# Block 0's gate moves its split halves to the MLP ring; the norms of blocks 2 and 3 are woven into the stages before the MLP; two key buffers and larger rings of small tiles

## The chip, the cores and the metric

The kernel runs on one core of a Trainium2 chip. The metric is device microseconds of one execution. A core has a matrix engine (PE, with its weight loads shown apart as PEld), three engines for elementwise work (VectorE: DVE, ScalarE: ACT, GpSimd: POOL) and a queue that issues all of this kernel's data transfers (SyncE: SP). Each of them works through its own list of instructions strictly in the order in which the list was written; they meet only in semaphore waits. On-chip memory (SBUF) holds tiles of 128 partitions; PSUM holds matmul results.

## What is computed

One layer of a streaming encoder for 2048 prompt frames and 32 sample frames of width 1024: an RMS norm, one input projection, two kinds of attention, an output projection with a residual, an MLP, a gate, a final norm. The part that the change touches:

```python
oa = diff_core(q, k, v, bias, mask, lam)    # 4 heads, two maps of 64 dims, softmax over all earlier keys
h = h + concat(oa, ob) @ w_out              # "outproj"
c = rmsnorm(h, g_mlp)                       # "cnorm", its row factor r is "colnorm"
h = h + square(relu(c @ w_up)) @ w_down     # "mlp"
h = h + sigmoid(h @ w_ple_gate) * (p @ w_ple_proj)   # "gate"
y = rmsnorm(h, g_final)                     # "final"
```

All of it is in 32-bit floats. Every matmul operand is split into a high part in the matrix engine's own 32-bit format and a remainder in the same format, and each product is made of three matmuls (high by high, high by low, low by high).

## The kernel before, in words

Activations lie transposed (features on partitions, tokens along the free side). The 2080 tokens are cut into four blocks: 0, 1 and 2 of 512 tokens, 3 of 544 in two pieces of 272. Blocks 0 and 1 make the first half, 2 and 3 the second. Intermediate results go through device memory: `kS` (split keys), `qS`, `oT` (attention output), `xT` (the input), `hS` (the residual stream after the output projection), `rS` (the row factors of the norm).

Weights come through `wunit` (L177): one transfer into a raw tile `wr` (a ring of two buffers), a copy to the high part `wh` on ACT (L169), a subtraction for the low part `wl` on POOL in four pieces of 256 columns (L164, L154), with rings of three. `split` (L165) does the same to activations; `mm3` (L185) issues the three matmuls per term, on L190, L191 and L192.

The order of the work. The Python text emits instructions in program order, with generators woven into each other by `weave` (one step of a side job after each step of the main job). A planner then lists the instructions of each engine: it goes through a simulated time, and whenever an engine is free it takes the ready instruction that stands first in the program. What it lists is fixed before the run. Where a transfer on the chip takes longer than the planner took it to take, the engine waits at that place of its list although later entries could run. Tiles of one tag share a ring of `bufs` buffers.

The stages that matter here, in program order:

- `attn_a` for the key groups `JA1` (L512). For each of four heads (g) it loads the keys of that head into `ka` (one buffer of 2208 columns, two maps; six transfers), and then works through the query pairs j: (4, 5) for all four heads, and then (6, 7, 8) for all four; j = 8 is the sample, whose 160 keys are the last columns of `ka`. Scores `s` come from L567.
- The MLP of blocks 0 and 1 (`mlp`, L976), which stands behind the attention in the program, and which the planner puts into the places where the matrix engine would wait for the attention. `oload(2)` (L822) reads and splits the attention output of block 2 into the 16 buffers of the ring `up`, and can start when the attention's memory is free.
- `gate(1)` (L996) and `final(1)`.
- `outproj(2)` (L844) woven with `oload(3)`; `outproj(3)`, with the row factor of block 2 (`colnorm`, L889) after its first step. A step of `outproj` is one weight unit: it loads `hd` from `xT`, adds the matmul result (L860), squares it on ACT (L865), adds the squares on POOL, and stores `hd` to `hS`. `hd`, the squares, the raw attention output and the raw rows of the norm all share the tag `tmp`, a ring of four.
- `gate(0)`: its split of h lies in two large tiles `hH`, `hL` of the ring `act` (four large tiles in all, which the split attention output of block 3 and the normed blocks 2 and 3 also use). After its first step the row factor of block 3 is made.
- `cnorm(2)`, `cnorm(3)` (L870): load r back from `rS`, and for each of eight row groups load `hS`, scale (DVE, L881), and split (copy on ACT, low part on POOL or DVE in turn) to `cH`, `cL`.
- The MLP of blocks 2 and 3 with `final(0)` between; its first part computes for each of two column groups f the blocks 2 and 3 (`mlp_up`, L917). Then the last gates and norms.

Of the kernel before, what the change touches and what calls it, by code (L numbers as in the profile page):

```python
# [19 lines left out]
P = 128  # L20
D = 1024
# [61 lines left out]
def drain(gen):  # L83
    for _ in gen:
        pass
# [48 lines left out]
class Kern:  # L134
    def __init__(self, tc, a):
        self.tc = tc
        self.nc = tc.nc
        self.a = a

    def dma(self, dst, src):  # L140
        if dst.dtype == F32R:
# [34 lines left out]

    def wunit(self, src, shape, hi_eng="act", lo_eng="pool"):  # L177
        nc = self.nc
        raw = self.wp.tile([P] + shape, F32, tag="wr", bufs=2, name="wr")
        self.dma(raw, src)  # L180
        hi = self.wp.tile([P] + shape, F32R, tag="wh", bufs=3, name="wh")
        lo = self.wp.tile([P] + shape, F32R, tag="wl", bufs=3, name="wl")
        self.split(hi, lo, raw, hi_eng, lo_eng)
        return hi, lo
# [326 lines left out]
    def attn_a(self, js, pool, ps_s, ps_t, ps_o):  # L511
        nc = self.nc  # L512
        last = 8 in js
        nk = KC if last else 256 * (js[-1] + 1)
        for g in range(4):
            ba = self.bias_a(pool, g)
            kt = pool.tile([P, 2, 1024 if self.small else KC], F32R, tag="ka", bufs=1, name="ka")
            for hl in range(2):
                src = self.kS[g, hl].rearrange("(m r) c -> r m c", m=2)
                for c0 in range(0, nk, 1024):  # L520
                    c1 = min(c0 + 1024, nk)
                    self.dma(kt[64 * hl : 64 * hl + 64, :, c0:c1], src[:, :, c0:c1])
            for j in js:
                self.attn_a_pair(g, j if j < 8 else None, kt, ba, pool, ps_s, ps_t, ps_o)

    def attn_a_pair(self, g, j, kt, ba, pool, ps_s, ps_t, ps_o):
        nc = self.nc
# [9 lines left out]
        for qi, t in enumerate(tiles):  # L537
# [25 lines left out]
            for bi, (k0, n, near) in enumerate(blocks):  # L563
                for m in range(2):
                    s = ps_s.tile([P, 512], F32, tag="s", name="s")[:nr, :n]
                    for hl in range(2):
                        nc.tensor.matmul(  # L567
                            s, q[:, m, hl, P * qi : P * qi + nr], kt[:, m, k0 : k0 + n], start=hl == 0, stop=hl == 1
                        )
                    dst = e[m][:nr, k0 - kb : k0 - kb + n]  # L570
                    nmx = nm[:nr, m, bi : bi + 1]
                    if near is None:
                        nc.vector.tensor_reduce(nmx, s, axis=AX.X, op=ALU.max, negate=True)  # L573
                        src = s
                    else:
                        nc.vector.tensor_tensor_reduce(
                            dst, s, ba[:nr, near : near + n], 1.0, -3e38, ALU.add, ALU.max, nmx
                        )
                        nc.vector.tensor_scalar(nmx, nmx, -1.0, None, op0=ALU.mult)
                        src = dst  # L580
                    nc.scalar.activation(dst, src, AF.Exp, bias=nmx, accum_out=z[:nr, m, bi : bi + 1])  # L581
# [218 lines left out]
                self.dma(self.pS[:, 1, k, t0 : t0 + n], lo[:, :n])  # L800

    def raw_o(self, wk, k, t0, n):
        t = wk.tile([P, BLK], F32, tag="tmp", bufs=4, name="oraw")[:, :n]
        self.dma(t, self.oT[:, k, t0 : t0 + n])
        return t

# [34 lines left out]
    def outproj(self, b, wk, oact, ps, acc):  # L841
        nc, a = self.nc, self.a
        n, t0 = BN[b], 512 * b
        W = a["w_out"][0]  # L844
        sq = wk.tile([P, BLK], F32, tag="acc", bufs=2, name="sqacc2")[:, :n]
        acc.append(sq)
        for d in range(8):
            wh, wl = self.wunit(W[:, P * d : P * d + P].rearrange("(k p) c -> p k c", p=P), [8, P])
            h = wk.tile([P, BLK], F32, tag="tmp", bufs=4, name="hd")[:, :n]
            self.dma(h, self.xT[:, d, t0 : t0 + n])  # L850
            for s0, sn in SUBS[b]:
                p = ps.tile([P, 512], F32, tag="mm", name="ops")[:, :sn]
                self.mm3(
                    p,
                    [
                        (wh[:, k], wl[:, k], oact[0][k][:, s0 : s0 + sn], oact[1][k][:, s0 : s0 + sn])
                        for k in range(8)
                    ],
                )
                nc.vector.tensor_tensor(h[:, s0 : s0 + sn], h[:, s0 : s0 + sn], p, op=ALU.add)  # L860
            if d == 0:
                nc.scalar.activation(sq, h, AF.Square)
            else:
                tmp = wk.tile([P, BLK], F32, tag="tmp", bufs=4, name="tmp")[:, :n]
                nc.scalar.activation(tmp, h, AF.Square)  # L865
                self.pool_tt(sq, sq, tmp, ALU.add)
            self.dma(self.hS[:, d, t0 : t0 + n], h)
            yield

    def cnorm(self, b, wk, act, out):  # L870
        nc = self.nc
        n, t0 = BN[b], 512 * b
        cH = act.tile([P, 8, act.aw], F32R, tag="act", name="cH")
        cL = act.tile([P, 8, act.aw], F32R, tag="act", name="cL")
        out[b] = (cH, cL)
        r = wk.tile([P, BLK], F32, tag="r", bufs=2, name="rl")[:, :n]
        self.dma(r, self.rS[:, t0 : t0 + n])
        for k in range(8):
            tmp = wk.tile([P, BLK], F32, tag="tmp", bufs=4, name="tmp")[:, :n]
            self.dma(tmp, self.hS[:, k, t0 : t0 + n])  # L880
            nc.vector.scalar_tensor_tensor(  # L881
                tmp, tmp, self.g_mlp[:, k : k + 1], r, op0=ALU.mult, op1=ALU.mult
# [34 lines left out]
    def mlp_up(self, ch, nf, blocks, st, wk, up, mm):  # L917
        nc = self.nc
        Wu = self.a["w_up"][0]
        us = {}  # L920
        for f in range(nf):
            ft = nf * ch + f
            wh, wl = self.wunit(Wu[:, P * ft : P * ft + P].rearrange("(k p) c -> p k c", p=P), [8, P])
            for b in blocks:
                h, cH, cL = st[b]
                uh = up.tile([P, up.aw], F32R, tag="u", name="uh")
                ul = up.tile([P, up.aw], F32R, tag="u", name="ul")
                us[f, b] = (uh, ul)
                for s0, sn in SUBS[b]:
                    ps = mm.tile([P, 512], F32, tag="mm", name="ups")[:, :sn]  # L930
                    self.mm3(
                        ps,
                        [(wh[:, k], wl[:, k], cH[:, k, s0 : s0 + sn], cL[:, k, s0 : s0 + sn]) for k in range(8)],
                    )
                    r = wk.tile([P, BLK], F32, tag="tmp", bufs=4, name="relu")[:, :sn]
                    nc.scalar.activation(r, ps, AF.Relu)  # L936
                    nc.scalar.activation(r, r, AF.Square)
                    self.split(uh[:, s0 : s0 + sn], ul[:, s0 : s0 + sn], r, "act", "pool")
        return us

    def mlp_down(self, ch, nf, blocks, us, st, wk, mm):
# [43 lines left out]
        self.gf = pool.tile([P, D], F32, name="gf")  # L985
        self.dma(self.gf, self.a["g_final"].unsqueeze(0).broadcast_to([P, D]))

    def gate(self, b, h, up, act, md):
        nc, a = self.nc, self.a
        n, t0 = BN[b], 512 * b  # L990
        Wg, Wp = a["w_ple_gate"][0], a["w_ple_proj"][0]
# [1 line left out]
        for i in range(2):  # L993
            for k in range(2):
                self.dma(pT[i][k][:, :n], self.pS[:, i, k, t0 : t0 + n])
        hH = act.tile([P, 8, act.aw], F32R, tag="act", name="hH")  # L996
        hL = act.tile([P, 8, act.aw], F32R, tag="act", name="hL")
        for k in range(8):
            self.split(hH[:, k, :n], hL[:, k, :n], h[:, k, :n], "act", "dve" if k % 2 else "pool")
        for dq in range(2):  # L1000
            ph, pl = self.wunit(
                Wp[:, 512 * dq : 512 * dq + 512].rearrange("(k p) c -> p k c", p=P), [2, 512]
# [1 line left out]
            for d4 in range(4):  # L1004
                d = 4 * dq + d4
                wh, wl = self.wunit(Wg[:, P * d : P * d + P].rearrange("(k p) c -> p k c", p=P), [8, P])
                for s0, sn in SUBS[b]:
                    pg = md.tile([P, 512], F32, tag="mm", name="gps")[:, :sn]
                    self.mm3(
                        pg,  # L1010
                        [(wh[:, k], wl[:, k], hH[:, k, s0 : s0 + sn], hL[:, k, s0 : s0 + sn]) for k in range(8)],
                    )
                    sg = up.tile([P, BLK], F32, tag="u", name="sig")[:, :sn]
                    sm = up.tile([P, BLK], F32, tag="u", name="sm")[:, :sn]
                    nc.scalar.activation(sg, pg, AF.Abs)
                    nc.vector.tensor_scalar(sm, pg, 0.0, None, op0=ALU.min)
                    nc.scalar.activation(sg, sg, AF.Exp, scale=-1.0)
# [78 lines left out]
    def run(self):  # L1096
        tc, nc, a = self.tc, self.nc, self.a
        with ExitStack() as top:
# [8 lines left out]
            cp = opened(top, "cp", 1)  # L1107
            self.dp = opened(top, "dp", 1, bass.MemoryType.DRAM)
            self.wp = opened(top, "wp", 3)
            mm = opened(top, "mm", MM, PSUM)  # L1110
            tp = mm
            psx = ExitStack()
# [84 lines left out]
                weave(self.outproj(1, wk, oa[1], mm, acc[1]), norms(0, actq, mm), 1, 1)  # L1197
            hq = opened(sq_, "hq", 1)
            uq = Sized(opened(sq_, "uq", 8), 512)
            up = Sized(opened(top, "uh", 16, side="right"), BLK)  # L1200
            oxs = ExitStack()
            ox = opened(oxs, "ox", 1, side="right")

# [21 lines left out]
            psx.close()  # L1225
            wk = opened(top, "wk4", 1)
            fk = opened(top, "fk4", 1)
            self.gfin(fk)
            md = opened(top, "md", 8 - MM, PSUM, "right")
            act = Sized(opened(top, "acth", 4), BLK, True)  # L1230
# [1 line left out]
            weave(self.outproj(2, wk, oa[2], md, acc[2]), self.oload(3, wk, act, oa), 1, 0, OW)  # L1232
            g = self.outproj(3, wk, oa[3], md, acc[3])
            next(g)
            self.colnorm(acc[2][0], 2, 1.0 / D, wk, mm, "mm", self.rS)
            drain(g)
            h = hload(hh, BLK, 0)
            g = self.gate(0, h, up, act, md)
            next(g)
            self.colnorm(acc[3][0], 3, 1.0 / D, wk, mm, "mm", self.rS)  # L1240
            drain(g)
            for b in HALVES[1]:
                drain(self.cnorm(b, wk, act, cn))
            f = self.final(0, h, up, fk, mm)
            st = {b: (hload(hh, BLK, b),) + cn[b] for b in HALVES[1]}
            m = self.mlp(HALVES[1], st, wk, up, mm, md)
# [59 lines left out]
```

## Time and profile before

| what | value |
|---|---|
| median of 3 runs | 3257.93 us (3256.7 to 3264.15) |
| the profiled execution's own time | 3256.49 us |
| its span, first to last instruction | 3254.6 us |
| granted matrix-engine clock, mean | 0.984 |
| PE busy | 3076.7 us, 95% of the span |
| POOL, ACT, DVE busy | 52%, 52%, 48% |
| DMA moved | 489 MB, mean 150 GB/s |
| key attention `JA1` with the MLP of blocks 0 and 1 | about 1260 to 2100 us |
| gate(1), final(1), outproj(2), outproj(3), gate(0), norms | about 2109 to 2374 us |
| MLP of blocks 2 and 3 | about 2359 to 3115 us |

The span and the execution's time differ by 1.9 us, which lies before the first and after the last instruction. A line of a wait table reads: engine, what it was about to do and its line, what released it, the total in us, how many times, and the longest. A line of a table by windows gives the stretch, its length, and the busy time and instruction count of PE, PEld, DVE, ACT and POOL, then the mean granted clock, the DMA share and GB/s. A timeline line gives start, length, engine, line, operation, output and inputs, count, and in brackets the idle time before it with its releaser. Times on "issue" are those where the profile shows no releaser.

### The profile page before, as it was taken

The page shows a single profiled execution, that of the slowest core. Times are in us where ns is not written, and L with a number is a line of the kernel's source. Part 1 is how long each engine was busy: PE and PEld are TensorE (multiplying, and loading weights), DVE is VectorE, ACT ScalarE, POOL GpSimd, SP SyncE. Part 2 cuts the span into 40 slices and gives each one's busy share as a digit, 9 for nine tenths or more (in the row PEclk, how much of TensorE's full clock was granted, in tenths as well). Part 3 has the DMA queues.
Part 4 walks back from the last instruction along what each step waited for, and adds up shares of the span by engine and source line. Part 5 has one row for each costly group of instructions (what it writes and reads, how often), then busy time and mean ns, then how long its engine had stood idle before and what let it go on. Part 6 is the DMA issues. An engine that isn't in the chain of part 4 may idle for free. (4 is left out here: it accounts for less than half of the span.)

```text
span 3254.6 us, 51557 instructions
## 1 busy us (share of the span) xinstructions
PE 3076.7 (95%) x17881; PEld 2692.7 (83%) x17881; DVE 1557.3 (48%) x3952; ACT 1693.7 (52%) x3717; POOL 1706.8 (52%) x2515
## 2 busy tenths in 40 slices
PE   6998999899999999999999999989899999999998
PEld 6877789789987887878788788868789999999988
DVE  5116786544465554676664565625442232223235
ACT  4226666776666765676665566544443222322245
POOL 5446766233245544565655455676854333433387
PEclk9999999999999999999999999999999999999999
DMA  7488786786788654554644544347531111111133
GB/s 232 165 259 246 226 244 206 213 259 202 215 239 229 187 146 118 152 156 138 199 122 135 137 123 136 121 143 233 150 113 46 46 46 46 46 46 46 47 94 103
DMA packets 519085, 489.02 MB, mean 150 GB/s; under 512 B 37885, under 2 KB 414017, under 8 KB 518825
## 3 DMA queue, kind: packets, MB, share of 16 engines
q1 hardware_dynamic: 518824, 485.73, 50.9%
q8 instruction: 142, 2.33, 0.3%
q14 instruction: 119, 0.97, 0.1%
HBM read 379.06 MB, written 110.49 MB: 150 GB/s over the span
## 5 line engine op out<-in xcount | busy, mean ns | idle before, releaser
L164 POOL TENSOR_TENSOR wl<-wr,wh 128x256 fp32r<-128x256 f32 x936 | 695.2, 774 | 489.4 <-ACT wh L169 453.1
L169 ACT ACTIVATE wh<-wr 128x1024 fp32r<-128x1024 f32 x338 | 357.2, 1057 | 598.5 <-PE dps L191 298.9
L971 DVE TENSOR_TENSOR h<-h,dps 128x512 f32<-128x512 f32 (+1 forms) x640 | 373.0, 585 | 575.0 <-PE dps L192 562.7
L154 POOL TENSOR_TENSOR wl<-wr,wh 128x256 fp32r<-128x256 f32 x416 | 301.8, 757 | 401.2 <-ACT wh L169 386.9
L190 PE MATMUL dps<-uh,wh 128*128 128x512 f32 (+1 forms) x1280 | 458.2, 358 | 7.1 <-DVE h L971 5.8
L190 PE MATMUL ups<-cH,wh 128*128 128x512 f32 (+1 forms) x1280 | 452.7, 354 | 5.7 <-ACT relu L936 4.5
L191 PE MATMUL ups<-cL,wh 128*128 128x512 f32 (+1 forms) x1280 | 451.5, 353 | 1.5 <-POOL cL L154 1.2
L192 PE MATMUL ups<-cH,wl 128*128 128x512 f32 (+1 forms) x1280 | 450.8, 352 | 0.0
L192 PE MATMUL dps<-uh,wl 128*128 128x512 f32 (+1 forms) x1280 | 450.1, 352 | 0.0
L191 PE MATMUL dps<-ul,wh 128*128 128x512 f32 (+1 forms) x1280 | 449.3, 351 | 0.0
L154 POOL TENSOR_TENSOR ul<-relu,uh 128x136 fp32r<-128x136 f32 (+1 forms) x320 | 198.9, 643 | 171.0 <-ACT uh L169 166.7
L190 PEld LDWEIGHTS dps<-uh,wh 128*128 128x128 f32 x1280 | 241.6, 189 | 39.7 <-DVE h L971 10.2
L190 PEld LDWEIGHTS ups<-cH,wh 128*128 128x128 f32 x1280 | 241.1, 188 | 38.6 <-ACT relu L936 4.7
L191 PEld LDWEIGHTS ups<-cL,wh 128*128 128x128 f32 x1280 | 241.6, 189 | 33.0 <-POOL cL L154 2.0
L192 PEld LDWEIGHTS dps<-uh,wl 128*128 128x128 f32 x1280 | 240.9, 188 | 33.6
L192 PEld LDWEIGHTS ups<-cH,wl 128*128 128x128 f32 x1280 | 241.3, 189 | 30.0
L191 PEld LDWEIGHTS dps<-ul,wh 128*128 128x128 f32 x1280 | 241.9, 189 | 26.5
L190 PE MATMUL qps<-aH,wh 128*128 128x512 f32 (+1 forms) x640 | 229.7, 359 | 11.0 <-ACT kr L432 3.4
L192 PE MATMUL qps<-aH,wl 128*128 128x512 f32 (+1 forms) x640 | 228.0, 356 | 0.0
L191 PE MATMUL qps<-aL,wh 128*128 128x512 f32 (+1 forms) x640 | 227.9, 356 | 0.0
L567 PE MATMUL s<-ka,q 128*128 128x256 f32 (+4 forms) x784 | 191.7, 346 | 30.8 <-DMA ka<-kS 10.1
L581 ACT ACTIVATE e<-s,nm 128x512 f32<-128x512 f32 (+3 forms) x256 | 154.9, 611 | 80.3 <-DVE nm L573 69.4
(218 smaller groups left out, 7075.0 us busy)
## 6 DMA issues: line engine op xcount, KB each, us to landing
wr<-w_up SPq DMA_DIRECT2D x96, 512.0 KB, 4.2
wr<-w_down SPq DMA_DIRECT2D x96, 512.0 KB, 3.8
wr<-w_in SPq DMA_DIRECT2D x74, 512.0 KB, 5.1
q<-qS SPq DMA_DIRECT2D x256, 128.0 KB, 4.3
v<-vSa SPq DMA_DIRECT2D x64, 512.0 KB, 3.9
ka<-kS SPq DMA_DIRECT2D x32, 512.0 KB, 7.7
wr<-w_out SPq DMA_DIRECT2D x32, 512.0 KB, 4.7
wr<-w_ple_gate SPq DMA_DIRECT2D x32, 512.0 KB, 4.4
```

The lines of the kernel that those rows point to most:

```text
L154: nc.gpsimd.tensor_tensor(out[:, sl], a[:, sl], b[:, sl], op=op)
L164: nc.gpsimd.tensor_tensor(out[:, sl], a[:, sl], b[:, sl], op=op)
L169: nc.scalar.activation(hi, raw, AF.Copy)
L190: nc.tensor.matmul(ps, lh, rh, start=start and i == 0, stop=False)
L191: nc.tensor.matmul(ps, lh, rl, start=False, stop=False)
L192: nc.tensor.matmul(ps, ll, rh, start=False, stop=stop and i == n - 1)
L567: nc.tensor.matmul(s, q[:, m, hl, P * qi : P * qi + nr], kt[:, m, k0 : k0 + n], start=hl == 0, stop=hl == 1)
L581: nc.scalar.activation(dst, src, AF.Exp, bias=nmx, accum_out=z[:nr, m, bi : bi + 1])
L971: nc.vector.tensor_tensor(hv, hv, ps, op=ALU.add)
```

## The change

- Keys: `ka` holds 2048 columns instead of 2208 and has two buffers in the second attention stage; the sample's 160 keys get a tile of their own, `ks` (one buffer). The number of transfers and their bytes stay.
- `gate(0)` puts its split of h into 16 tiles of the ring `up`, which grows from 16 to 20 buffers; its two scratch tiles per step (`sig`, `sm`) come from the ring `tmp`. The other gates are as they were.
- `cnorm(2)` is woven into `outproj(3)` and `cnorm(3)` into `gate(0)`, one row group after each step. Their row factor r is used where it lies: the store to `rS` and the load back are gone.
- The first chunk of each MLP goes through the column groups of one block before the next block (it changes something only where two blocks are done together, in the second half).
- In the second half the ring `tmp` has eight buffers instead of four, and raw weights alternate between the old ring of two and another ring of two in the work pool.

```diff
+            kt = pool.tile([P, 2, 1024 if self.small else SP], F32R, tag="ka", bufs=1 if self.small else 2, name="ka")
+            if last:
+                ks = pool.tile([P, 2, PAST + SS], F32R, tag="ks", bufs=1, name="ks")
...
+                if last:
+                    self.dma(ks[64 * hl : 64 * hl + 64], src[:, :, SP:KC])
...
+                self.attn_a_pair(g, j if j < 8 else None, kt if j < 8 else ks, ba, pool, ps_s, ps_t, ps_o)
...
-    def cnorm(self, b, wk, act, out):
+    def cnorm(self, b, wk, act, out, r=None):
...
-        r = wk.tile([P, BLK], F32, tag="r", bufs=2, name="rl")[:, :n]
-        self.dma(r, self.rS[:, t0 : t0 + n])
+        if r is None:
+            r = wk.tile([P, BLK], F32, tag="r", bufs=2, name="rl")[:, :n]
+            self.dma(r, self.rS[:, t0 : t0 + n])
...
+        us, w = {}, {}
+        order = [(f, b) for f in range(nf) for b in blocks]
+        if ch == 0:
+            order = [(f, b) for b in blocks for f in range(nf)]
+        for f, b in order:
...
+            hH, hL = [[up.tile([P, BLK], F32R, tag="u", name="hu")[:, :n] for k in range(8)] for _ in range(2)]
...
+                         else wk.tile([P, BLK], F32, tag="tmp", bufs=self.nt, name=x))[:, :sn]
...
+            self.rawp = Rings((self.wp, "wr"))
...
-            up = Sized(opened(top, "uh", 16, side="right"), BLK)
+            up = Sized(opened(top, "uh", 20, side="right"), BLK)
...
+            self.nt = 8
+            self.rawp = Rings((self.wp, "wr"), (wk, "wr"))
...
             g = self.outproj(3, wk, oa[3], md, acc[3])
             next(g)
-            self.colnorm(acc[2][0], 2, 1.0 / D, wk, mm, "mm", self.rS)
-            drain(g)
+            r = self.colnorm(acc[2][0], 2, 1.0 / D, wk, mm, "mm", None)
+            weave(g, self.cnorm(2, wk, act, cn, r), 1)
             h = hload(hh, BLK, 0)
-            g = self.gate(0, h, up, act, md)
+            g = self.gate(0, h, up, act, md, wk)
             next(g)
-            self.colnorm(acc[3][0], 3, 1.0 / D, wk, mm, "mm", self.rS)
-            drain(g)
-            for b in HALVES[1]:
-                drain(self.cnorm(b, wk, act, cn))
+            r = self.colnorm(acc[3][0], 3, 1.0 / D, wk, mm, "mm", None)
+            weave(g, self.cnorm(3, wk, act, cn, r), 1)
```

## The prediction, made before the changed kernel was run

> **What bounds the kernel now.** I read the page's busy line first, then the matrix engine's table of waits, then tables by windows and timelines around the longest waits.
>
> ```profile
> PE 3076.7 (95%) x17881; PEld 2692.7 (83%) x17881; DVE 1557.3 (48%) x3952; ACT 1693.7 (52%) x3717; POOL 1706.8 (52%) x2515
> ```
>
> PE bounds the kernel, and the change removes no matmul. So it can win only idle time (3254.6 - 3076.7 = 178 us) and time at a lowered clock. Where that lies, by windows:
>
> ```profile
> 1260.00:2100.00 840.00, 804.37 (x4081) 677.07 (x4080) 510.66 (x1135) 521.79 (x1203) 463.57 (x658) 0.99 0.51 141
> 2288.00:2359.00 71.00, 59.24 (x245) 47.51 (x246) 33.39 (x40) 34.23 (x55) 63.46 (x81) 0.93 0.48 146
> 2405.00:3120.00 715.00, 715.00 (x4429) 648.38 (x4428) 209.28 (x405) 205.47 (x354) 285.98 (x448) 1.00 0.17 52
> ```
>
> The attention stage idles 35.6 us; gate(0) idles 11.8 of 71, with POOL busy 63.5; the last MLP idles nowhere, so nothing can be won there. PE's waits, over the span:
>
> ```profile
> PE s L567 <- DMA ka<-kS: 10.1, 5, 3.6
> PE s L567 <- issue: 9.6, 2, 6.8
> ```
>
> and between 2100 and 2420 us:
>
> ```profile
> PE gps L190 <- ACT wh L169: 11.8, 2, 10.5
> PE gps L190 <- DVE sm L1016: 7.7, 5, 4.6
> PE ops L190 <- DVE hd L860: 6.5, 3, 4.1
> PE ups L190 <- ACT relu L936: 4.5, 1, 4.5
> ```
>
> The waits on "issue" turn out to be keys too. In a timeline, the sample's scores (32 rows) are the last readers of the old keys, and the six key loads follow at once:
>
> ```profile
> 1700.88 0.31 PE L567 MATMUL s<-ka,q 128*32 128x160 f32 x2
> 1701.29 5.10 SPq L145 DMA_DIRECT2D ka<-kS  x6
> 1713.90 0.70 PE L567 MATMUL s<-ka,q 128*128 128x512 f32 x2 [2.86 <-issue]
> ```
>
> 12.7 us pass between the last score of one head and the first of the next; the MLP covers 9.8 of them. After such waits the granted clock is down (stretch around a key wait, around gate(0)'s long wait):
>
> ```profile
> 1425.00:1433.00 8.00, 4.35 (x14) 3.31 (x13) 6.42 (x12) 1.70 (x4) 1.83 (x3) 0.79 1.07 221
> 2316.00:2334.00 18.00, 7.48 (x23) 5.67 (x22) 16.64 (x20) 7.37 (x12) 16.61 (x18) 0.72 0.58 180
> ```
>
> 8 x (1 - 0.79) = 1.7 us of work are lost behind a 3.65 us wait; behind the 10.5 us wait it is 18 x 0.28 = 5.0 us, about half of it while PE idled anyway, so 2.5.
>
> **The change, part by part.**
>
> *Two key buffers.* A head's keys can be loaded while the head before is worked on. Idle time on keys in this stage: 3.65 + 2.03 + 2.86 + 1.82 + 6.75 + 1.22 = 18.3 us (the 10.1 above has 1.4 of an earlier stage, which keeps its one buffer). Three of these waits end in a lowered clock, 1.7 us each: 23.4 in all. I take 21, since the first head of the stage has nothing to prefetch behind. Bounds: 0, if other waits take over, and 23.4. The loads are the same six per head; on SP's queue they only move ahead of q and v loads that are due later. `ks` has one buffer, so its load waits for the sample's scores of the head before; these lie a whole head back (80 to 120 us by the spacing of the loads), so nothing is queued behind it for long.
>
> *What follows from it.* The attention now ends at 2098 us, and `oload(2)` falls into gate(1): eight ACT copies (0.63 us), eight DVE remainders (1.2) and four DVE scalings (1.1) from 2110 to 2125, with `sm` of the gate behind them on DVE. That is the 4.62 us wait on `sm` at 2116.7 and 1.7 of clock. Seven head changes at up to 12.7 us would end the attention up to 80 us sooner; 15 suffice to clear gate(1). I take 5 of 6.3; bounds 0 and 6.3.
>
> *Eight buffers in `tmp`, four raw weights, split h out of the way.* In outproj(2) POOL did hL for 7.5 us (2222.6 to 2230.1) ahead of a weight's low part, and then PE waited for `hd`, whose load waited for a ring buffer: 0.54 + 4.11 + 0.73 + 0.66 + 1.71 = 7.8 us, and 1.7 of clock. The split of h now needs buffers of `up` that outproj(2) reads to its end, so it can't come there any more: it lies in outproj(3). SP's queue stood behind raw weights too:
>
> ```profile
> SPq L145 <- POOL wl L164: 69.8, 30, 4.7
> wr<-w_out SPq DMA_DIRECT2D x32, 512.0 KB, 4.7
> ```
>
> I take 7 of 9.5; bounds 0 and 9.5. Against it: the new raw ring lies, by the order in which tags are first used, over the memory of gate(1)'s split h. So the second weight of outproj(2) can be loaded only after gate(1)'s last matmul (2180.5), lands 4.7 us later, and its copy takes 1.06: about 2187.6 with the issues in front of it, while PE needs it at about 2185.5. Cost 2 to 4 us, the rest of final(1)'s transposes beside it; I take 3 (bounds 0 and 6).
>
> *The norms woven in.* Sixteen steps move; each is one load of `hS`, a DVE scaling (1.13 to 1.19 us), an ACT copy (0.63 to 0.65) and a remainder on POOL or DVE. Gone are two stores to `rS`, two loads, and the place where both norms stood behind the gate. What this stage loses now: 10.52 + 1.27 in gate(0), because a weight's copy stood on ACT behind four `cH` copies that came late:
>
> ```profile
> 2322.79 0.63 ACT L169 ACTIVATE cH<-tmp 128x512 fp32r<-128x512 f32 x1 [4.78 <-DVE tmp L881]
> 2327.41 1.04 ACT L169 ACTIVATE wh<-wr 128x1024 fp32r<-128x1024 f32 x1
> ```
>
> plus 2.5 of clock (14.3); and 4.49 + 0.67 + 0.59 + 0.93 = 6.7 with 1.7 of clock (8.4) at the MLP's start, which waits for `cH` of block 3. The second goes: with block 2's two column groups first, block 3 is wanted 11 us after the gate's end, when one or two steps are left. I take 7 of 8.4 (bounds 0 and 8.4). The first goes in part: the four copies of cnorm(2) leave, but cnorm(3) comes, with its row factor made in the same place on DVE. I take 10 of 14.3 (bounds 0 and 14.3), before the POOL cost that follows.
>
> *POOL.* The rows between 2173 and 2405 us:
>
> ```profile
> L164 POOL TENSOR_TENSOR wl<-wr,wh 128x256 fp32r<-128x256 f32 x112 | 87.2, 810 | 21.6 <-ACT wh L169 16.2 <-PE ops L192 5.4
> L154 POOL TENSOR_TENSOR sqacc<-sqacc,tmp 128x256 f32<-128x256 f32 x14 | 9.9, 730 | 7.4 <-ACT tmp L865 7.4
> L154 POOL TENSOR_TENSOR cL<-tmp,cH 128x256 fp32r<-128x256 f32 x8 | 7.9, 1014 | 0.0
> ```
>
> outproj(3): eight weights x 2.83 + seven additions x 1.64 + hL 7.5 + cL(2) 7.9 = 49.5 us, against PE's eight steps x 5.34 (spacing of the stores of `hd`) = 43. gate(0): ten weights x 2.83 + eight x (1.44 + 1.43) + cL(3) 7.7 = 59, against PE's eight x 7.0 = 56. POOL is over by 9.5 us in the sum, and by 19 if weights take 810 ns a piece instead of 707 and the gate's pieces 870 instead of 720. Against that stand the two weights that POOL is ahead by at the start (5.7) and the last two cL(3), after the gate (3.9). So 0 to 9.4; I take 10, above that, since the list's order will not be perfect and each wait costs clock as well.
>
> The same 128x256 form takes POOL 1014 ns beside DVE's norm steps and 730 elsewhere. If every DVE instruction that reads two SBUF tiles stopped POOL for its whole length, the two stages would have 36 of them (16 scalings, 12 remainders, 8 of the row factors) at 0.69 us, an undisturbed DVE addition of 512 columns: 25 us, a POOL term of 35 and a sum of 3244 (rival 2). The Trainium skill's page "SBUF — State Buffer", section "Who interferes with whom", states this rule, an exclusive lock between the two engines; the two durations agree in kind, not in size.
>
> *The other edits.* `sig` and `sm` in `tmp`, and 16 tiles instead of two large ones, issue the same instructions: 0, hidden while the ring of eight has room (three tiles a step, so over two steps ahead; without that room a step's `sm` waits for a norm step, 3 to 4 us).
>
> Sum: -21 - 5 - 7 + 3 - 10 - 7 + 10 = -37. Against the profiled execution's 3256.5: 3219.5, so 3220. The median of the runs is 1.4 us above it, which I leave out. A difference of 0.3% (10 us) is about what a measurement of this kernel can tell.
>
> **The rivals.**
>
> 1. *POOL takes back what the second half wins.* For it: 63.5 of 71 us busy in gate(0) before anything is added. Against: its slack in outproj(2). The keys and `oload(2)` stay, 26 us, 3 are lost: 3256.5 - 23 = 3233.
> 2. *DVE stops POOL, whole instructions long*, as worked out above: 3244. Against: POOL's mean in the window of the norms before is up by 15% (810 to 707), not by half.
> 3. *The keys' waits turn into others* (ACT and DVE at 510 to 522 of 840 us have room, which speaks against), the second half as forecast: 3256.5 + 3 - 14 = 3246.
> 4. *Slower: norm steps stall ACT's list.* The place is the `wh` copy behind `cH` behind a late `hS` load, as at 2322, but now at up to 15 woven steps. It decides from (37 + 10) / 15 = 3.1 us of PE idle a step; at 4.5 us a step, the time is 3219.5 + 68 = 3287. For it: one such place cost 10.5 us. Against: eight buffers let a load go ahead by two steps (14 us), and a load lands in about 4.
> 5. *The larger key tiles don't fit beside the MLP.* Tile shapes give 16384 more bytes per partition in the attention stage; if these lay over the MLP's buffers, the MLP could not fill the attention's gaps, and hundreds of us would be lost (3500). By my sum of the shapes it fits closely.
> 6. *A new plan loses elsewhere what this wins*, within 10 us of before: 3257. The gaps of 0.4 to 3 us all over the attention stage show how a plan misses.
>
> **How the numbers follow.** Forecast 0.52 (own range 3200 to 3232), rival 1 0.13, rival 2 0.04, rival 3 0.08, rival 4 0.11, rival 5 0.02, rival 6 0.10. Faster by over 0.3% (below 3247): 0.52 + 0.13 + 0.04 + 0.08 = 0.77; within: 0.10; slower: 0.13. The lower end, 3198, is all gains whole (61.9 us) less the late raw weight (3), with no POOL cost. The upper end, 3256, leaves out rivals 4 and 5 and half of 6, about 0.18.
>
> **What would show it.** Right: no PE wait on `ka` in the second attention stage; the six loads a head early; `ou` copies before gate(1)'s first matmul; no `hd` wait in outproj(2); `cH` of block 3 within gate(0); PE's waits in gate(0) ending on `wl` of POOL rather than on `wh` of ACT. Wrong: a PE wait on `wh` behind `cH` in several steps, or the attention's end still near 2098.

## The result, and the profile after

The changed kernel takes 3228.39 us (median of 4 runs, 3221.28 to 3235.92) beside 3257.31 us (4 runs, 3256.5 to 3264.15) for the kernel before on the same chip: a ratio of 0.9905, with a 95% interval of 0.9885 to 0.9925. Taken on another chip it was 3225.31 us beside 3260.06 us, 0.9903 (0.9886 to 0.9919). By the ratio it is faster by some 31 us; the forecast was 3220 us, 37 us faster. One profiled execution, that of the experiment `rings`, ran at a mean granted clock of 0.909, where the others that do the whole computation had 0.980 to 0.988, and its stage times are not used below.

The profiled execution that follows took 3235.92 us, the longest of its four, with a span of 3234.1 us. Its busy line:

```profile
PE 3085.2 (95%) x17881; PEld 2700.2 (83%) x17881; DVE 1548.9 (48%) x3952; ACT 1694.8 (52%) x3717; POOL 1711.0 (53%) x2515
```

Every engine issues as many instructions as before. PE is busy 8.5 us longer, although it multiplies the same; that is time at half clock, taken up at the end of this section. The table by windows of after, for the stages whose windows stand in the prediction (length; busy time and count of PE, PEld, DVE, ACT, POOL; clock; DMA share; GB/s):

```profile
1270.00:2090.00 820.00, 797.46 (x4056) 669.66 (x4055) 505.57 (x1129) 521.24 (x1202) 462.66 (x651) 0.99 0.51 145
2283.00:2344.00 61.00, 58.63 (x255) 46.45 (x254) 26.28 (x37) 31.93 (x52) 56.21 (x77) 1.00 0.41 126
2405.00:3095.00 690.00, 690.00 (x4285) 626.34 (x4284) 199.50 (x380) 194.71 (x332) 275.20 (x431) 1.00 0.16 48
```

PE now idles 22.5 us in the attention stage where it idled 35.6, and in gate(0) 2.4 of 61 us where it idled 11.8 of 71. POOL is still busy 92% of gate(0), but PE hardly waits for it. PE's waits of after in the attention stage, from its first score to its end:

```profile
PE dps L191 <- DVE h L981: 8.8, 9, 2.6
PE dps L191 <- ACT wh L170: 5.2, 1, 5.2
PE s L572 <- DMA q<-qS: 1.9, 2, 1.1
```

No wait on `ka` and none on "issue" is left (18.3 us before). Something took their place: the wait on `wh` is new, and that on `h` stood in the same stage of before as

```profile
PE dps L190 <- DVE h L971: 5.8, 6, 2.3
```

The timeline around the head change at 1710 shows the loads:

```profile
1605.77 2.96 SPq L146 DMA_DIRECT2D ka<-kS  x4
...
1708.53 0.31 PE L572 MATMUL s<-ks,q 128*32 128x160 f32 x2
1710.10 0.31 PE L572 MATMUL s<-ks,q 128*32 128x160 f32 x2
1710.52 1.26 SPq L146 DMA_DIRECT2D ks<-kS  x2
...
1712.63 0.70 PE L572 MATMUL s<-ka,q 128*128 128x512 f32 x2 [0.79 <-DMA q<-qS]
1714.41 3.06 SPq L146 DMA_DIRECT2D ka<-kS  x4
```

The keys that PE reads at 1712.63 were asked for at 1605.77, a whole head earlier, and at 1714.41 those of the next head are. From the end of the sample's last score to the next head's first there are 2.2 us, where 12.7 us passed before. PE's waits of after from 2080 to 2400 us:

```profile
PE gps L191 <- DVE sm L1033: 7.7, 5, 4.6
PE ops L191 <- ACT oact L170: 3.7, 2, 2.2
PE pps L191 <- DVE sm L1033: 2.8, 1, 2.8
PE ops L191 <- ACT wh L170: 2.0, 1, 2.0
PE gps L193 <- POOL wl L165: 1.2, 1, 1.2
PE ups L191 <- ACT relu L946: 1.1, 1, 1.1
...
PE gps L191 <- ACT wh L170: 0.6, 1, 0.6
```

The 11.8 us of `gps` on `wh` are down to 0.6, and `ops` no longer waits for `hd`. The waits on `sm` in gate(1) stand as they stood, 4.6 us for the longest.

To see where the time went, I cut both spans at the same instructions of PE: the first score of the second attention stage, the first `gps` of gate(1), the first `ops` of outproj(2), the first `gps` of gate(0), the first `ups` of the last MLP, and the first `gps` of the last gate. The idle time of PE within a stage stands in brackets. The second execution of after is the one profiled on the other chip; `keys` (the key edit alone) and `nokeys` (the change without it) are the first two experiments.

| stage, us (PE idle) | before | after | after, 2nd | keys | nokeys |
|---|---|---|---|---|---|
| up to the attention | 1273.8 | 1284.2 | 1271.3 | 1273.9 | 1277.0 |
| attention with MLP 0, 1 | 835.8 (34.5) | 820.9 (21.5) | 819.5 (21.5) | 818.5 (22.5) | 834.0 (32.5) |
| gate(1), final(1) | 63.2 (10.5) | 62.9 (10.4) | 63.6 (10.6) | 63.6 | 63.7 |
| outproj(2), outproj(3) | 116.3 (9.1) | 115.8 (6.3) | 111.8 (5.5) | 115.2 | 112.7 |
| gate(0), norms before | 69.7 (10.5) | 59.6 (2.4) | 60.7 (3.2) | 68.3 | 60.3 |
| MLP 2, 3 | 756.8 (6.7) | 751.6 (3.1) | 752.1 (3.1) | 758.9 | 752.2 |
| rest | 139.0 | 139.0 | 139.0 | 139.0 | 139.0 |

The stages that the change touches are 31.0 us shorter in after and 34.1 us shorter in its second execution. The first stage, 10.4 us longer in the one and 2.5 us shorter in the other, is no part of the change: the lists of ACT, POOL and DVE there (1754, 941 and 2130 instructions from the start) are the same in both kernels, and in all the experiments that do the whole computation. These two windows of the whole first stage, of before and then of after, show the difference as busy time of PE:

```profile
0.00:1273.80 1273.80, 1181.00 (x7289) 1042.11 (x7289) 655.68 (x2124) 753.83 (x1750) 626.39 (x941) 0.98 0.73 213
```

```profile
0.00:1284.20 1284.20, 1192.98 (x7290) 1053.92 (x7290) 652.03 (x2124) 754.80 (x1750) 626.78 (x941) 0.97 0.72 211
```

12 us more for the same matmuls at a lower clock. The longest stretch at half clock in after lasts 17.07 us, at 621 us; at the same place before has 6.83.

### The profile page after: what moved, and what is told of

It is laid out like the page before. It is cut to its first block, busy times and chain, and to the rows that moved or that the text cites. A ratio compares the mean times of both kernels' runs of the same rounds, so it can differ in the third digit from the quotient of the medians.

```text
span 3234.1 us, 51430 instructions
## 1 busy us (share of the span) xinstructions
PE 3085.2 (95%) x17881; PEld 2700.2 (83%) x17881; DVE 1548.9 (48%) x3952; ACT 1694.8 (52%) x3717; POOL 1711.0 (53%) x2515
## 3 DMA queue, kind: packets, MB, share of 16 engines
q1 hardware_dynamic: 518248, 484.65, 50.9%
## 5 line engine op out<-in xcount | busy, mean ns | idle before, releaser
L572 PE MATMUL s<-ka,q 128*128 128x512 f32 (+3 forms) x768 | 184.8, 342 | 12.2 <-DMA q<-qS 4.5
```

Source lines behind the costliest of these rows:

```text
L572: nc.tensor.matmul(s, q[:, m, hl, P * qi : P * qi + nr], kt[:, m, k0 - kb : k0 - kb + n], start=hl == 0, stop=hl == 1)
```

## The experiments

### Each half alone: `keys` and `nokeys`

`keys` is the kernel before with the key edit alone, `nokeys` the changed kernel without it:

```diff
-            kt = pool.tile([P, 2, 1024 if self.small else KC], F32R, tag="ka", bufs=1, name="ka")
+            kt = pool.tile([P, 2, 1024 if self.small else SP], F32R, tag="ka", bufs=1 if self.small else 2, name="ka")
+            if last:
+                ks = pool.tile([P, 2, PAST + SS], F32R, tag="ks", bufs=1, name="ks")
...
```

> The kernel before with the key edit alone (two buffers of ka, the sample's keys in ks). My theory, that the two halves of the change add up: the attention stage is 15 us shorter (its length from the first score of the stage to gate(1) 835.8 before, 820.9 in the changed kernel), the rest as before, so about 15 us or 0.5% faster. Rival, that the key buffers only pay together with the second half: within 5 us of before. Rival, that the attention's end limits gate(1) (what I had forecast): 21 to 26 us faster, with the attention's last matmul at least 15 us ahead of gate(1)'s first.

> The changed kernel with one key buffer as before. My theory: 16 us (0.5%) faster than before: gate(0) 10 us shorter, the MLP's start 5, outproj(2) and outproj(3) together unchanged at 116; the key waits of the attention stage are back. Rival, that the larger rings shorten the attention stage too (they are opened after it, but the planner could differ): over 20 us faster.

Measured: `keys` 3241.65 us (5 runs), ratio 0.9947 (0.9926 to 0.9968); `nokeys` 3240.52 us (4 runs), 0.9947 (0.9929 to 0.9964). The kernel before had 3261.14 us on that chip. So the halves win about 17 us each by these ratios, and 0.9947 x 0.9947 = 0.9894 lies within the interval of the whole: they add. In `keys` the 17.3 us come from the attention stage alone. PE's waits of `keys` from 2080 to 2400 us still have the losses of the second half:

```profile
PE gps L190 <- ACT wh L169: 10.7, 2, 9.7
PE gps L190 <- DVE sm L1020: 7.8, 5, 4.8
...
PE ups L190 <- ACT relu L940: 4.5, 1, 4.5
```

The line on `sm` is the one that the forecast let go with an earlier end of the attention; here the keys have come early, and it stands.

### What the rings do without the norms: `rings`

Before, with eight buffers in `tmp` and the second raw-weight ring, and nothing else:

```diff
...
+            self.nt = 8
+            self.rawp = Rings((self.wp, "wr"), (wk, "wr"))
...
```

> The kernel before with the larger rings alone in the second half (eight small tiles, raw weights in two rings of two), nothing woven, h split as before. Rival theory, that depth of buffers is what frees gate(0): gate(0) at 60 us instead of 70, 10 us faster in all. My theory, that the weaving takes cnorm(2) out of gate(0) and that this frees ACT's list: gate(0) stays at 66 to 70 us, outproj(2) and outproj(3) gain 0 to 5, the total is within 6 us of before.

Measured: 3249.97 us (10 runs), 0.9981 (0.9961 to 1.0001), so about 6 us, with an interval that touches no change and reaches up to 13 us. By the ratios, more buffers alone bring some third of the 17 us that the whole second half wins in `nokeys`. Without its stage times, whether they shorten gate(0), as the rival in the expectation has it, stays open.

### The norms not woven: `noweave`

```diff
-            weave(g, self.cnorm(2, wk, act, cn, r), 1)
+            drain(g)
+            r2 = r
...
-            weave(g, self.cnorm(3, wk, act, cn, r), 1)
+            drain(g)
+            drain(self.cnorm(2, wk, act, cn, r2))
+            drain(self.cnorm(3, wk, act, cn, r))
```

> The changed kernel with both norms drained behind gate(0) instead of woven in (row factors made in the same places, all else as changed). If the weaving carries the second half's gain: gate(0) and the MLP's start lose 10 to 15 us against the changed kernel, 3256 - 15 = 3241 in all. If the rings and the free large tiles carry it (the planner pulls the norms forward by itself, since their tiles are free): within 4 us of the changed kernel, 3225 to 3230.

Measured: 3240.96 us (4 runs), 0.9945 (0.9928 to 0.9962), 0.4% or 13 us worse than the change. Gate(0) is as short without the norms in it: 61.0 us, of which the last 4.3 are already the wait for `cH`. Its own matmuls take 56.7 us with 0.3 of idle time, less than with the norms woven in (59.6 and 2.4 in after). But the last MLP takes 765.4 us (751.6 in after), since PE now waits for the norms at its start. Of PE's waits from 2080 to 2400 us in this kernel:

```profile
PE ups L192 <- POOL cL L155: 6.9, 1, 6.9
PE ups L191 <- ACT relu L946: 4.6, 1, 4.6
PE ups L191 <- ACT cH L170: 4.3, 1, 4.3
```

15.8 us on `cH`, `cL` and what follows from them. So it is not weaving that shortens gate(0). In before, the copies to `cH` of block 2 stand in gate(0) from 2309 to 2327 us; here the first comes at 2335.3, behind the gate's last matmul. Which of the other edits moved them there is not shown. Weaving is what keeps that gain from being given back one stage later.

### The order of the last MLP's first chunk: `forder`

The changed kernel with the old order, block by block within a column group:

```diff
-        if ch == 0:
-            order = [(f, b) for b in blocks for f in range(nf)]
```

> The changed kernel, but with the blocks of the first hidden chunk of the last MLP in the order of before. If that order carries the earlier start of the last MLP, the stage of the last MLP (751.6 us) gets 3 to 7 us longer. If the woven norms alone carry it, the stage stays within 2 us.

Measured: 3227.5 us (4 runs), 0.9906 (0.9891 to 0.992), beside 3225.31 us and 0.9903 for the changed kernel on the same chip. The totals do not tell the two apart. The stage does: the last MLP takes 756.7 us, 4.6 us longer than in the second execution of after, with PE idle 6.3 us (3.1) and one more half-clock stretch. Of PE's waits from 2080 to 2400 us in this kernel:

```profile
PE ups L191 <- ACT relu L944: 1.9, 1, 1.9
PE ups L191 <- ACT cH L170: 1.8, 1, 1.8
PE ups L192 <- POOL cL L155: 1.0, 1, 1.0
```

Block 3 is wanted early, before its last row groups are split. So the MLP's start needs both: norms woven in, and block 2's groups first.

### Is POOL the limit of the second half? `allpool`

All low parts of the two woven norms go to POOL, where half went to DVE. This takes eight subtractions of 544 or 512 columns from DVE and puts them on the engine that the forecast thought full:

```diff
-            self.split(cH[:, k, :n], cL[:, k, :n], tmp, "act", "dve" if k % 2 else "pool")
+            self.split(cH[:, k, :n], cL[:, k, :n], tmp, "act", "pool" if b > 1 or k % 2 == 0 else "dve")
```

> The changed kernel with all remainders of the norms of blocks 2 and 3 on POOL, eight more of 1.4 to 1.8 us each. If POOL is the limit of gate(0) (57.9 of 59.6 us busy there): gate(0), outproj(3) or the MLP's start lose 6 to 12 us. If POOL only looks full because it works ahead, and PE waits for it nowhere: within 4 us of the changed kernel.

Measured: 3225.53 us (4 runs), 0.9898 (0.9878 to 0.9918), no slower than the change. PE's longest wait in gate(0) and at the MLP's start is, by the table from 2270 to 2400 us,

```profile
PE gps L191 <- ACT wh L170: 4.9, 2, 3.3
```

not one on `wl` of POOL, although POOL is busy 57.3 of 60 us there:

```profile
2278.00:2338.00 60.00, 55.14 (x233) 44.15 (x232) 30.25 (x32) 33.53 (x55) 57.30 (x81) 0.97 0.39 112
```

So an engine that is busy 95% of a stage need not be what the stage waits for. Quite free the extra work is not: the wait of 3.3 us is for a `wh` copy that stands on ACT behind two copies to `cH`, which is rival 4's mechanism; PE idles 4.9 us in gate(0) and 3.9 in the last MLP, where it idled 3.2 and 3.1 in the second execution of after. The medians do not show it.

### The attention without the MLP beside it: `lone1` and `lone2`

Why did the attention not end far earlier, when the time from head to head fell by 10 us? Both kernels leave out the MLP of blocks 0 and 1, so that only the attention is left in the stage; `lone1` has one key buffer, `lone2` two:

```diff
...
-                m = self.mlp((b,), {b: (h,) + cn[b]}, wk, uq, mm, mm)
+                m = iter(())
...
```

> The changed kernel with one key buffer, and with the MLP of blocks 0 and 1 left out, so that the attention of the second key stage stands alone. If a pair's own chain (scores, maximum, exponential, transposes, products) sets the attention's pace and the key load is late besides: the stage runs near 800 us without the MLP too. If the MLP's instructions between slow the attention: clearly shorter, 500 to 650 us.

> The same with two key buffers. What I had forecast (each of seven head changes leaves the attention 12.7 us without work): 60 to 90 us shorter than with one buffer. If the key load lies beside the tail of the head before (its last transposes and products), so that two buffers only take the last part of the wait: 15 to 35 us shorter.

Measured: 2873.18 and 2854.02 us (one run each). From the first score to the last product the attention takes 586.0 us with one buffer and 572.6 with two. The 60 to 90 us that I had expected between them are 13.4. Two waits of `lone1` between 1222 and 1800 us are those of the keys,

```profile
PE s L568 <- issue: 13.4, 3, 5.2
PE s L568 <- DMA ka<-kS: 5.3, 2, 2.9
```

18.7 us together, at the first five head changes; the last two end in waits on the queries of 5.3 and 4.8 us. In `lone2` the key waits are gone, but these two lines stand there (a wait on the values was 1.5 us before):

```profile
PE s L572 <- DMA q<-qS: 15.9, 3, 5.5
PE o L658 <- DMA v<-vSa: 13.3, 4, 4.8
```

The three waits on queries are those of the three head changes that follow a sample. In `lone1`, 15.4 to 16.3 us pass there from the last score of a head to the first of the next, and PE idles 8.6 to 9.5 of them; products of the old head fill the rest. In `lone2` 5.2 to 5.5 us pass, all of them idle. So even without an MLP a large part of a head change was work, and of the idle part some 5 us only change their reason, from the keys to the queries: the seven head changes cost 28.8 us of waits in `lone1` and 15.9 in `lone2`, 12.9 of the 13.4 us. And 573 to 586 us of attention take 805 to 821 us when the MLP lies in the same stage. That how the planner lays the MLP into the attention sets its end, much more than the keys, fits these figures, but no run varied that layout.

### Can the wait on `sm` in gate(1) be woven away? `gate1w`

The loads and splits of block 2's attention output (`oload(2)`) are woven into gate(1), two of them per step, where the program had all of them before the gate:

```diff
-                    drain(self.oload(2, ox, up, oa))
-                    oxs.close()
...
-            drain(self.gate(1, h, uq, actq, mm))
+            weave(self.gate(1, h, uq, actq, mm), self.oload(2, ox, up, oa), 1, 0, 2)
+            oxs.close()
```

> The changed kernel with the load and split of block 2's attention output woven into gate(1), two steps after each of its steps, instead of standing ahead of it. If these splits are what makes the gate's minimum late on DVE (the wait of 4.65 us and a clock stretch, not removed by the change): gate(1) 5 to 7 us shorter, 0.2% faster than the changed kernel. If the wait has another cause: gate(1) stays at 63 us; if outproj(2) now waits for the splits: it loses 2 to 6.

Measured: 3226.95 us (4 runs), 0.9903 (0.9886 to 0.992): no change. The wait stayed, at 5.5 us. DVE's timeline in this kernel shows why:

```profile
2101.03 3.52 DVE L176 TENSOR_TENSOR ou<-oraw,ou 128x512 fp32r<-128x512 f32 x3
2105.48 3.33 DVE L840 SCALAR_TENSOR_TENSOR oraw<-oraw,g_b_s,rb 128x512 f32<-128x512 f32 x3 [0.93 <-DMA oraw<-oT]
2108.73 0.68 DVE L1033 TENSOR_SCALAR sm<-gps 128x512 f32<-128x512 f32 x1
2109.33 0.73 DVE L840 SCALAR_TENSOR_TENSOR oraw<-oraw,g_b_s,rb 128x512 f32<-128x512 f32 x1
```

Weaving sets only the rank. The gate's first product was done at 2103.99, but three scalings of the raw attention output, for whose transfer DVE idles until 2105.48, stand ahead of its `sm` on the list. By the planner's rule they must have been ready, in its simulated time, before that product was.

### The late raw weight: `rawlate`

The new raw ring is used from outproj(3) on only:

```diff
-            self.rawp = Rings((self.wp, "wr"), (wk, "wr"))
...
+            self.rawp = Rings((wk, "wr"), (self.wp, "wr"))
             g = self.outproj(3, wk, oa[3], md, acc[3])
```

> The changed kernel itself, beside the next three on one chip. It should stand at about 0.9905 of before (some 3228 us). Its unchanged first stage (before attention of block 2) tells how far the clock's half-speed stretches move one execution: 1273.8 us in the profile of before, 1284.2 us in that of after, with the same instructions.

> The changed kernel, but the second raw-weight ring in use only from the out projection of block 3 on. If the second weight of outproj(2) comes late (a 1.99 us wait and a half-clock stretch behind it, 3.4 us long and so 1.7 us) because its raw buffer lies in memory that gate(1)'s split h holds to the end, this wait goes and the out projections lose 2 to 4 us: some 3225 us. If the weight is late for another reason, for one that its copy has to queue on ScalarE, the time is that of the changed kernel within 2 us.

Measured: 3223.68 us (4 runs), 0.9892 (0.9878 to 0.9907), beside 0.9903 (0.9886 to 0.9919): 1.6 us less, within the intervals. In the profile the wait at the second weight of outproj(2) (1.1 to 2.3 us in seven executions with the ring in use from the start) is gone, and the out projections take 110.0 us (111.8 on the same chip). So the cause, a buffer that lies over gate(1)'s split h, is borne out. Its price is not resolved by the time: 1.8 us in the stage, just below the 2 to 4 expected, and gate(0) is 2.0 us longer in the same profile (62.7 us).

### A better version: `best`

`gate1w` had left the wait on `sm` to the order of DVE's list. The other way is to let PE go on while the first evictions are late. Gate(1) has the ring `mm` of two accumulators; gate(0) has six. `best` is `rawlate` with the scores' banks closed earlier, so that gate(1) can use the six:

```diff
-            drain(self.gate(1, h, uq, actq, mm))
-            psx.close()
+            psx.close()
+            md = opened(top, "md", 8 - MM, PSUM, "right")
+            drain(self.gate(1, h, uq, actq, md))
...
```

> The changed kernel with the late raw ring, and with gate(1)'s matmuls in the six-bank accumulator ring that gate(0) uses, the scores' banks being closed before it. If gate(1)'s waits on the products' evictions (4.65 and 2.75 us, and five of about 0.8 us) come from too few accumulators, the stage of gate(1) loses 6 to 10 us and the whole 8 to 14 us: some 3215 us. If they come from the order of VectorE's work, whose splits of the attention output stand ahead of the first evictions, the first wait of 4 to 5 us stays and no more than 4 us are won.

Measured: 3214.9 us (4 runs, 3213.55 to 3215.53), 0.9864 (0.9849 to 0.9879), below the change's 0.9903 with no overlap, and 45 us below the kernel before. The stage of gate(1) lasts 60.1 us with PE idle 1.6 (63.8 and 11.0 in `rawlate`), and no half-clock stretch is left in it. This stage by windows, of after and then of `best`:

```profile
2105.10:2168.00 62.90, 52.47 (x212) 41.10 (x211) 22.33 (x27) 28.89 (x43) 47.14 (x61) 0.95 0.51 162
```

```profile
2093.60:2153.80 60.20, 58.62 (x259) 47.62 (x257) 23.71 (x32) 32.77 (x51) 52.75 (x71) 1.00 0.57 180
```

PE records 259 matmuls in the stage instead of 212: with six accumulators all 240 products of gate(1) lie before the first one of outproj(2), where 30 of them came behind it in after, and so part of the gain shows in the next stage. (The other 17 are of the MLP and a norm, beside which the gate now starts.) Together the two stages take 167.0 us in `best`, 173.8 in `rawlate` and 175.4 in the second execution of after. In the table of `best`'s waits from 2080 to 2400 us `sm` does not occur. Its two longest are

```profile
PE ops L191 <- ACT oact L170: 6.0, 1, 6.0
PE gps L193 <- POOL wl L165: 2.2, 2, 1.2
```

and the first, in outproj(3), is what I would look at next. The wait on `sm` had two parents: an order of DVE's list that makes the first eviction late, and too few accumulators to work on meanwhile. `gate1w` did not change the first; `best` removes the second, and that is enough. The first eviction is even later there: `sm` starts 17.7 us after the gate's first matmul, against 11.5 us in `rawlate`, and PE works on meanwhile.

## Why the prediction was right, and where it was wrong

The time came out 8 us above the forecast, within its own range of 3200 to 3232, and the changed stages sum to -31 and -34 us in the two executions of after, against -37. The parts were less well sized than the sum.

- **Keys, -21.** The mechanism is shown: no wait on `ka` or issue, loads a head early, and the stage takes 815.8 to 820.9 us in nine profiled executions with two buffers, and 834.0 and 835.8 in two with one. That is some 16 us. All 18.3 us of key waits went, but waits on a weight and on `h` of the MLP (5.2 and 3.0 us more) came in their place, so PE's idle time fell by 13.0 us and the clock's loss by 2.9. The step that overrated it counted every key wait as won.
- **What follows from it, -5: wrong, it was 0.** The step was that a head change shortened by up to 12.7 us would end the attention up to 80 us sooner, with 15 enough to clear gate(1). The attention did end 15 us earlier within its stage (806.4 us after its start, not 821.3), but so did the MLP beside it, and gate(1) with them: the last product lies 14.5 us before gate(1) in both. `oload(2)` stayed where it was relative to the gate, and the wait on `sm` with it. `lone1` and `lone2` show that the head change was not worth 12.7 us even by itself: seven of them gave 13.4 us. The prediction had named the sign for this failure: the attention's end near 2098. It was 2090.6.
- **Rings and split h, -7, late raw weight, +3.** The out projections are 0.5 us shorter in the execution shown and 4.5 in the second, so the net of -4 lies at the upper end of what was won. The `hd` waits are gone; `oact` took 3.7 us. The late weight came as computed: the loads of outproj(2)'s second and third weights go out at 2176.28 and 2177.37, the copy starts at 2182.34, and PE waits 2.0 us. `rawlate` confirms the cause.
- **Norms woven, gate(0) -10.** It is 9.0 and 10.1 us shorter. But the reason was only half right: `noweave` with 61.0 says that the late copies are avoided as well by taking the norms out of that place altogether. **MLP start, -7:** the last MLP is 4.7 and 5.2 us shorter, and this needs weaving and the new block order together (`noweave`, `forder`).
- **POOL, +10: mis-sized, some 2.** In after PE waits for `wl` 1.2 us in gate(0) and 0.5 at the MLP's start. The sum of POOL's work in outproj(3) was right, 49.5 us forecast and 49.2 and 50.9 measured in the two executions; what it was set against was not. PE's step was taken as 5.34 us, from the stores of `hd`. The matmuls of five successive steps in before start at 2257.3, 2263.7, 2269.7, 2275.8 and 2281.8 us, 6.1 us apart, so eight steps take 49 us and not 43 (with their waits 56.9 and 55.1 in after): POOL was not over by 6.5 us there. In gate(0) it was busy 54.8 of 59.6 and 54.0 of 60.7 us, where 59 us of work in 56 were forecast.

```profile
L165 POOL TENSOR_TENSOR wl<-wr,wh 128x256 fp32r<-128x256 f32 x112 | 87.6, 817 | 14.7 <-ACT wh L170 14.7
...
L155 POOL TENSOR_TENSOR hu<-h,hu 128x256 fp32r<-128x256 f32 x8 | 9.5, 1205 | 0.0
```

  These are its rows from 2168 to 2405 us. Its largest wait there is for `wh` of ACT, so over the whole stretch POOL also waited for work, and `allpool` gave it more with no loss in the median. Taking a value above the worked-out 0 to 9.4 us for an imperfect list added to the error. The upper of these two figures was off too: it sets 810 ns, the mean length of a weight's piece, against 707, a quarter of the busy time of four; by busy time the prediction's row gives 779 (87.2 us for 112).

So two errors cancelled for the most part: some 10 us of gains that did not come, from the keys and from what follows, and 8 us of POOL's cost that did not come either. That the sum came out so close is luck to this extent.

**The rivals.** The second half (out projections, gate(0), last MLP) won 16 to 18 us, where the forecast's terms made it 11, rival 1 (POOL takes it back) a loss of 3 and rival 2 a loss of 14. Rival 2's mechanism, DVE stopping POOL, is treated in the last section. Rival 3: partly, 8 of 18.3 us. Rival 4, ACT's list stalled by norm steps, does not show: `gps` waits 0.6 us on `wh` in all of gate(0). In `allpool` it does with 4.9 us. Rival 5 does not show: attention and MLP overlap as before. Rival 6 falls with the ratio's interval.

## What to carry to other kernels

A wait that goes is replaced in part by whatever was next late in the same stretch, so take the idle time of the stage and its floor and not the sum of the waits; here 13 of 18 us remained won. When the consumer's evictions stand behind other work in an engine's fixed list, more accumulators can be worth more than an attempt to reorder that list: here six instead of two won 9 us (`best` beside `rawlate`), weaving nothing. Before a step is moved into a stage, compare where the waiting goes if it is only moved behind it: the move of the norms pays because of the MLP behind gate(0), not because of gate(0).

## What the runs showed of the hardware

**The clock's stretches differ from one execution to the next.** The same list of instructions up to the attention took 1271.3 to 1284.2 us in eleven profiled executions, with 20 to 37 us of matmul time lost at half clock. The stretches are 3.41 us long or multiples of it (but for the last, cut off by the program's end), and stand on a grid of 3.41 us. Three such windows of after:

```profile
2235.80:2239.20 3.40, 3.29 (x26) 3.06 (x25) 0.57 (x1) 0.00 (x0) 3.40 (x6) 1.00 1.02 338
2239.20:2242.60 3.40, 1.49 (x9) 1.27 (x10) 2.99 (x3) 1.21 (x2) 3.40 (x4) 1.00 1.00 335
2242.60:2246.00 3.40, 3.40 (x17) 3.40 (x16) 1.87 (x4) 1.61 (x2) 1.98 (x3) 0.50 1.05 348
```

A window in which PE was idle 1.9 of 3.4 us, most of it in waits of 1.53 and 0.49 us, is followed by one at half clock, in which PE loses 1.7 us of work. Laid on that grid, and counted from 20 us on in these eleven executions, the 215 windows at full clock that half clock followed were idle for at least 0.9 us, and windows with up to 1.9 us of idle time were still followed by full clock: between the two, the idle time alone does not decide. At half clock less is enough. The 204 windows that full clock followed were idle for at most 0.57 us, the 102 that another half followed for at least 0.32. The Trainium skill, page "TensorE: Matmul & The Clock Gate", section "What's actually happening", gives the window as 3413 ns, free-running, and the trace agrees; it says that the clock falls after an idle window of that length, while here 1.9 of its 3.4 us were enough. Where a wait of 2 us falls in the grid then decides whether it costs 2 or 3.7 us, which fits the spread. The stretch of 17.07 us fits the counts too: its first four windows are idle for 0.39 to 0.58 us, the fifth not at all.

**DVE and POOL slow each other where DVE reads two wide SBUF tiles.** From 2109 us on in after, three DVE splits of 512 columns stand beside POOL pieces of 256 columns:

```profile
2108.54 3.52 DVE L176 TENSOR_TENSOR ou<-oraw,ou 128x512 fp32r<-128x512 f32 x3
2109.18 8.24 POOL L165 TENSOR_TENSOR wl<-wr,wh 128x256 fp32r<-128x256 f32 x8
```

The three splits take 1.22 us each, and the first three pieces 1.17 to 1.19. Alone it is 685 ns for such a split (the mean of 20 with POOL idle) and 741 ns for a piece (the mean of 1652 with no DVE instruction of two SBUF inputs beside them). One after the other, a split and a piece would need 1.43 us; side by side they need some 1.2. So a piece loses 0.45 us to a wide split, not the split's whole 0.69 us that rival 2 counted. Narrow instructions cost nothing: 29 pieces with half a microsecond or more of DVE instructions of one column beside them took some 760 ns on average. The Trainium skill, page "SBUF — State Buffer", section "Who interferes with whom", has these two contend for an exclusive lock; the trace agrees that they contend, and here the loss is about two thirds of an instruction.
